# All four feed-forwards by seven block products in fixed steps, with modulation and norm work spread over three engines

## Chip, cores and metric

The kernel runs on one core of a Trainium2 chip. The metric is the device time of one execution in microseconds, median of three runs.

## What is computed

Two layers of a diffusion backbone run on 640 tokens (128 context, 512 latent) of width 1024. Cut to what matters here:

```python
def swiglu(h, w_gu, w_down):                 # w_gu 1024 x 5632, w_down 2816 x 1024
    g, u = jnp.split(h @ w_gu, 2, axis=-1)
    return (jax.nn.silu(g) * u) @ w_down
def run_layer(x, cond, lp, rope, ctx):
    mod = (jax.nn.silu(cond) @ lp['w_mod'] + lp['b_mod']).reshape(cond.shape[0], N_MOD, 1, D_MODEL)
    h = rmsnorm(x, nw[0]) * (1 + mod[:, 1]) + mod[:, 0]
    x = x + 0.5 * mod[:, 2] * swiglu(h, lp['ffn1_wgu'], lp['ffn1_wd'])
    h = rmsnorm(x, nw[1]) * (1 + mod[:, 4]) + mod[:, 3]
    out, new_ctx = token_mix(h, lp, rope, ctx)
    x = x + mod[:, 5] * out
    h = rmsnorm(x, nw[2]) * (1 + mod[:, 7]) + mod[:, 6]
    x = x + 0.5 * mod[:, 8] * swiglu(h, lp['ffn2_wgu'], lp['ffn2_wd'])
```

Each layer thus has a first feed-forward, a token mixer and a second feed-forward. The modulation vectors `mod` differ for context and latent tokens, so a segment boundary lies inside the first half of the tokens.

## The kernel before

Activations lie with features on the 128 partitions and tokens along the row, in two halves of 320 tokens; `HO = (1, 0)` makes half 1 (called p) the first and half 0 (called q, with the segment boundary) the second. Every float32 operand of a matmul is split in a rounded high part and the rest: ScalarE writes the high part (`act`), VectorE subtracts it to give the low part (`tt`), and three matmuls (high by high, high by low, low by high) stand for one product. Weights come as raw 128x512 tiles through three buffers `w`, and are split into seven pairs `wh`, `wl`.

Three of the four feed-forwards (both of layer 0, the first of layer 1) go through `ffn` (L427): two passes over 11 of the 22 hidden tiles each, gate and up projections first (8 input tiles by 3 matmuls for each of gate, up and token half), then the down projection. Beside them `mod_steps` (L348) computes modulation columns: 56 in the first feed-forward, 24 in the second, 48 in the third. A column is one 128x1024 weight row block, loaded by DMA, and two VectorE multiplications with an accumulated sum (L325, L328), one for context and one for latents. `spread` gives how many columns follow each step.

The last feed-forward goes through `ffn7` (L513). Its first `PLAIN = 2` hidden tiles are computed as above, with a down projection of their own. For the other 20, the input tiles, the two token halves and gate/up form 2x2 blocks, and seven block products of 12 matmuls each (P1, Q5, P2, Q6, Q3, Q7, Q4) take the place of eight. That needs sums of the inputs (`sums7`, on GpSimd) with their splits (`split7`), four GpSimd additions of 128x512 weights for each hidden tile, and recombinations on VectorE and ScalarE. The work is a list of steps of 12 matmuls (`order`): four hidden tiles, then a down projection of 16 steps over them, and so on. `put` hangs the work of the other engines on step numbers: a weight's load 8 steps and its split 5 steps ahead of its use. While `pin` is set, each engine keeps this program order; elsewhere a list scheduler orders instructions by its own estimate.

Between stages, `x_update` adds to the residual, `sq_tile` accumulates squares, and once the last output tile of a half is done, `norm_half` or `norm7_half` computes the reciprocal root (eight VectorE operations of 128x320) and then each of eight tiles (`norm_tile`: VectorE scale, ScalarE shift and rounding, VectorE remainder; two segments in half q). The last outputs are taken half by half (`TAIL`, `TAIL_O`), so that matmuls of q stand beside the norm of p. The tiles of class "B" are four slots of 656 values, which hold the full-precision normed half p (`xf`) and, later, two of the four raw weights of a hidden tile.

Of the kernel before, what the change touches and what calls it, by code (L numbers as in the profile page):

```python
# [104 lines left out]
class Trunk:  # L105
# [168 lines left out]
    def start(s, mc):  # L274
# [16 lines left out]
        s.h = [s.H() for _ in range(KT)]  # L291
        bm, nw = mc["sp"][:, S_OFF["bmod"][0]:S_OFF["bmod"][1]], mc["sp"][:, S_OFF["nw"][0]:S_OFF["nw"][1]]
        for f0 in range(0, KT, 4):
            fs = slice(f0, f0 + 4)
            for j in (1, 0):
# [6 lines left out]
                row = s.slots.alloc(512, False, "B")  # L302
# [13 lines left out]
            for h in HO:  # L316
                for f in range(f0, f0 + 4):
                    s.norm_tile(0, h, f, rs[h])

    def mod_cols(s, mc, j, f, pin=False):  # L320

        nc = s.nc
        l, m = mc["l"], mc["m"]
        cs = s.cs
        q = j * KT + f  # L325
        w = s.wm[q % 2]
        nc.sync.dma_start(out=w, in_=s.a["wmod"][l, q])
        i = s.stt(s.jk.ap, w, 0.5, cs[:, 0, :], ALU.mult, ALU.mult, accum_out=m[:, 0, q:q + 1])  # L328
        if pin:
            s.tc.keep_in_program_order(i)  # L330
        s.stt(w, w, 0.5, cs[:, 1, :], ALU.mult, ALU.mult, accum_out=m[:, 1, q:q + 1])
# [16 lines left out]
    def mod_steps(s, n):  # L348

        for _ in range(n):  # L350
            if s.todo:
                mc, j, f = s.todo.pop(0)
                s.mod_cols(mc, j, f, True)
                if f == KT - 1:
                    s.mod_fin(mc, j)
# [71 lines left out]
    def ffn(s, wgu, wd, i, mods, done):  # L427

        step = 0
        for hf in range(2):  # L430
            acts = [s.A(2 * T, True) for _ in range(NH)]
            w = {} if hf else {0: s.ahead}
            for mi, h in s.halves(NH, 0 if hf else HEAD, 0):
                m = hf * NH + mi
                if mi not in w:
                    w[mi] = [s.prep(wgu[m, n], KT) for n in range(2)]
                wg, wu = w[mi]
                av = acts[mi].v(2, r=True)
                sl = s.hs(h)
                g = s.proj(wg, h)  # L440
                u = s.proj(wu, h, ps=s.bank())
                t = s.norm.tile([P, H], F32, name="th", tag="tmp", bufs=4)
                s.act(t, g[:, :H], AF.Tanh, scale=0.5)
                s.stt(t, t, 1.0, g[:, :H], ALU.add, ALU.mult)
                s.tt(t, t, u[:, :H], ALU.mult)
                s.split(av[:, 0, sl], av[:, 1, sl], t)
                s.mod_steps(mods(step))
                step += 1
            if hf == 1:
                s.free(s.h)  # L450
            w = {}
            for o, h in s.halves(KT, 0, TAIL if hf else 0):
                if o not in w:
                    w[o] = s.prep(wd[o][:, hf * NH:hf * NH + NH, :], NH)
                sl = s.hs(h)
                ps = s.bank() if (2 * o + h) % 2 else s.wbank()
                s.mms(ps[:, :H], w[o], s.hl_of(acts, sl), NH)
                s.x_update(ps, i, o, h)
                if hf == 1:
                    done(o, h)  # L460
                s.mod_steps(mods(step))
                step += 1
            for a in acts:
                a.free()
# [5 lines left out]


    def norm7_half(s, i, h):

        p, q = HO
        if h == p:
            s.h = [s.H() for _ in range(KT)]
            s.xf = [s.slots.alloc(2 * H, False, "B").v(2) for _ in range(K2)]
        else:
            reg = [s.A(4 * H).v(2, 2) for _ in range(K2 // 2)]
            s.xq = [reg[k // 2][:, k % 2] for k in range(K2)]  # L480
        ps = s.bank()
        s.mm(ps[:, :H], s.ones, s.ss[h])
        r = s.norm_r(ps)
        for k in range(KT):
            t = s.norm_tile(i, h, k, r)
            f = (s.xf if h == p else s.xq)[k % K2][:, k // K2]
            for c, a, b in s.segs(h):
                o = slice(a - h * H, b - h * H)
                s.act(f[:, o], t[:, o], AF.Identity, bias=s.mB[:, c, i, k:k + 1])
# [31 lines left out]
    def ffn7(s, wgu, wd, i, mods, done):  # L521
        p, q = HO
        step = [0]

        def beside():
            s.mod_steps(mods(step[0]))
            step[0] += 1

# [3 lines left out]
        acts = [s.A(2 * T, True) for _ in range(PLAIN)]  # L532
        w = {0: s.ahead}
        n = 0
        for mi, h in s.halves(PLAIN, PLAIN, 0):
            if mi not in w:
                w[mi] = [s.prep(wgu[mi, e], KT) for e in range(2)]
            g = s.proj(w[mi][0], h)
            u = s.proj(w[mi][1], h, ps=s.bank())
            av, sl = acts[mi].v(2, r=True), s.hs(h)  # L540
            t = s.norm.tile([P, H], F32, name="th", tag="tmp", bufs=4)
            s.act(t, g[:, :H], AF.Tanh, scale=0.5)
            s.stt(t, t, 1.0, g[:, :H], ALU.add, ALU.mult)
            s.tt(t, t, u[:, :H], ALU.mult)
            s.split(av[:, 0, sl], av[:, 1, sl], t)
            if h == q:
                s.sums7(n)
                n += 1
            beside()
        w = {}  # L550
        per = WK // PLAIN
        for o in range(KT):
            if o % per == 0:
                r, (wh, wl) = s.raw(), s.hilo()
                for e in range(per):
                    s.nc.sync.dma_start(out=r[:, e * PLAIN:e * PLAIN + PLAIN, :], in_=wd[o + e][:, :PLAIN, :])
                s.split(wh, wl, r)
            for h in (q, p):
                ps = s.bank() if (2 * o + h) % 2 else s.wbank()
                xs = s.hl_of(acts, s.hs(h))  # L560
                for k in range(PLAIN):
                    e = o % per * PLAIN + k
                    s.three(ps[:, :H], (wh[:, e, :], wl[:, e, :]), xs(k), k == 0, k == PLAIN - 1)
                s.x_update(ps, i, o, h)
                beside()
            if o < K2:
                if n < K2:
                    s.sums7(n)
                    n += 1
                s.split7(o)  # L570
            else:
                k = o - K2
# [1187 lines left out]
```

## Time and profile before

| | us |
|---|---|
| runs (median, lowest, highest) | 3152.12, 3151.34, 3154.68 |
| the profiled execution, its time | 3150.53 |
| its span (first to last instruction) | 3148.7 |

The profile is one execution. An engine's busy time is the union of its instructions; matmuls overlap in the records, so a row of a matmul shows some 310 ns where the next one starts 147 ns later. Idle time of an engine that is not the bottleneck costs nothing. The stages, in us from the span's start, are: start to 52, first feed-forward to 517, mixer to 1145, second feed-forward to 1605, third to 2073, mixer to 2692, last feed-forward to the end.

### The profile page before, as it was taken

What the parts mean: (1) busy time and instruction counts of PE and PEld (TensorE: products, weight loads), DVE (VectorE), ACT (ScalarE), POOL (GpSimd) and SP (SyncE); (2) the same over time, 40 slices, a digit from 0 to 9 for tenths busy, and PEclk for the clock granted to TensorE, in tenths of its full rate; (3) what the DMA queues carried; (4) which work ended last, traced back from release to release, by engine and by line L of the source; (5) the groups of instructions that cost most, each with busy time, mean ns of one, the idle gap of its engine ahead of it and who ended that gap; (6) DMA issues with size and microseconds to landing.
All of it is one profiled execution on the core that took longest, in us unless ns stands there. A gap on an engine that the chain in (4) does not pass through costs nothing.

```text
span 3148.7 us, 54263 instructions
## 1 busy us (share of the span) xinstructions
PE 3087.9 (98%) x21206; PEld 2929.5 (93%) x21206; DVE 2136.4 (68%) x4268; ACT 1220.8 (39%) x2444; POOL 140.0 (4%) x118
## 2 busy tenths in 40 slices
PE   8999999999999999999999999999999999899999
PEld 5999998998887999999999999989989779799999
DVE  5667677757758774555566666676685687887776
ACT  4222223346544442222242223243464454444443
POOL 0000000000000000000000000000000000232221
PEclk9999999999999999999999999999999999999999
DMA  6445452454322422332323443434533224122222
GB/s 221 135 142 172 140 162 88 138 159 121 120 71 72 142 82 91 115 117 98 115 77 131 148 147 129 146 102 130 167 111 97 65 73 143 54 84 81 83 82 81
DMA packets 261468, 364.87 MB, mean 116 GB/s; under 512 B 97708, under 2 KB 143612, under 8 KB 260476
## 3 DMA queue, kind: packets, MB, share of 16 engines
q1 hardware_dynamic: 252572, 340.66, 34.1%
q10 hardware_dynamic: 8640, 20.76, 1.8%
q8 instruction: 166, 2.72, 0.4%
q14 instruction: 90, 0.74, 0.1%
HBM read 325.37 MB, written 35.96 MB: 115 GB/s over the span
## 4 chain that ended last, share of the span: by engine, by line
PE 89%; DVE 6%; ACT 3%; DMA 1%; issue 1%; SPq 0%; POOL 0%; DVEq 0%; ACTq 0%; POOLq 0%
PE wacc L188 47%; PE acc L188 42%; DVE tn L179 1%; ACT t_A L162 1%; DVE wl L171 1%; DVE t_H L179 1%; DVE t_S L1291 1%; DVE t_A L171 1%; ACT t_H L162 1%; ACT t_B L162 0%; DVE t_A L179 0%; ACT t_W L162 0%; DVE t L179 0%; ACT wh L162 0%; DMA w<-in_wd 0%
## 5 line engine op out<-in xcount | busy, mean ns | idle before, releaser
L188 PE MATMUL wacc<-t_H,wh 128*128 128x320 f32 x5248 | 1188.3, 312 | 24.5 <-ACT t_H L162 9.4
L188 PEld LDWEIGHTS wacc<-t_H,wh 128*128 128x128 f32 x5248 | 877.9, 187 | 52.5 <-DVE t_H L179 14.3
L188 PE MATMUL wacc<-t_H,wl 128*128 128x320 f32 x2624 | 812.3, 311 | 2.5 <-DVE wl L171 2.5
L162 ACT ACTIVATE wh<-w 128x512 fp32r<-128x512 f32 (+2 forms) x772 | 470.4, 613 | 746.5 <-PE wacc L188 488.3
L171 DVE TENSOR_TENSOR wl<-w,wh 128x512 fp32r<-128x512 f32 (+2 forms) x772 | 528.4, 686 | 251.0 <-ACT wh L162 245.1
L188 PE MATMUL acc<-t_H,wh 128*128 128x320 f32 x2496 | 556.6, 308 | 0.0
L188 PE MATMUL acc<-t_A,wh 128*128 128x320 f32 x2272 | 503.6, 308 | 0.2 <-DVE t_A L171 0.2
L188 PEld LDWEIGHTS wacc<-t_H,wl 128*128 128x128 f32 x2624 | 491.5, 187 | 10.3 <-issue 5.3
L188 PE MATMUL wacc<-t_A,wh 128*128 128x320 f32 x2048 | 468.2, 310 | 9.3 <-DVE tg L179 5.5
L188 PEld LDWEIGHTS acc<-t_H,wh 128*128 128x128 f32 x2496 | 418.5, 188 | 0.8 <-ACT wh L162 0.2
L188 PE MATMUL acc<-t_H,wl 128*128 128x320 f32 x1248 | 383.6, 308 | 0.0
L188 PEld LDWEIGHTS acc<-t_A,wh 128*128 128x128 f32 x2272 | 380.1, 188 | 0.8 <-DVE t_A L171 0.5
L188 PEld LDWEIGHTS wacc<-t_A,wh 128*128 128x128 f32 x2048 | 345.2, 188 | 17.3 <-DVE tg L179 6.6
L188 PE MATMUL acc<-t_A,wl 128*128 128x320 f32 x1136 | 350.0, 308 | 0.3 <-DVE wl L171 0.3
L188 PE MATMUL wacc<-t_A,wl 128*128 128x320 f32 x1024 | 317.3, 310 | 2.0 <-DVE wl L171 2.0
L188 PEld LDWEIGHTS acc<-t_H,wl 128*128 128x128 f32 x1248 | 234.0, 188 | 0.1
L188 PEld LDWEIGHTS acc<-t_A,wl 128*128 128x128 f32 x1136 | 213.3, 188 | 0.5 <-DVE wl L171 0.5
L179 DVE SCALAR_TENSOR_TENSOR t_A<-acc,mG,t_A 128x320 f32<-128x320 f32 (+1 forms) x192 | 88.4, 479 | 178.8 <-PE acc L188 173.7
L188 PEld LDWEIGHTS wacc<-t_A,wl 128*128 128x128 f32 x1024 | 192.5, 188 | 5.2 <-DVE wl L171 2.2
L171 DVE TENSOR_TENSOR th<-th,acc 128x320 f32<-128x320 f32 x136 | 66.0, 487 | 186.9 <-PE acc L188 186.9
L162 ACT ACTIVATE t_A<-th 128x320 fp32r<-128x320 f32 x176 | 82.7, 471 | 248.4 <-DVE th L171 221.6
L179 DVE SCALAR_TENSOR_TENSOR t_W<-t_W 128x1024 f32<-128x1024 f32 x128 | 156.3, 1221 | 2.1
(201 smaller groups left out, 3086.0 us busy)
## 6 DMA issues: line engine op xcount, KB each, us to landing
w<-in_wgu SPq DMA_DIRECT2D x292, 256.0 KB, 2.8
t_W<-in_wmod SPq DMA_DIRECT2D x128, 512.0 KB, 4.1
w<-in_win SPq DMA_DIRECT2D x168, 256.0 KB, 3.0
w<-in_wd SPq DMA_DIRECT2D x136, 256.0 KB, 2.8
gd<-tg SPq DMA_DIRECT2D x96, 160.0 KB, 2.2
tg<-gd SPq DMA_DIRECT2D x96, 160.0 KB, 2.3
t_B<-in_wgu SPq DMA_DIRECT2D x40, 256.0 KB, 2.8
w<-in_wd SPq DMA_DIRECT2D x48, 192.0 KB, 2.4
```

The source lines that it names most:

```text
L162: return s.order(s.nc.scalar.activation(out=out, in_=in_, func=func, **kw))
L171: return s.order(s.nc.vector.tensor_tensor(out=out, in0=a, in1=b, op=op))
L179: return s.order(s.nc.vector.scalar_tensor_tensor(out=out, in0=a, scalar=sc, in1=b, op0=op0, op1=op1, **kw))
L188: return s.order(s.nc.tensor.matmul(out, lhsT, rhs, start=start, stop=stop, **kw))
L1291: nc.vector.tensor_reduce(out=nm2.ap[:, i:i + 1], in_=ps[:, :H], axis=AX.X, op=ALU.max)
```

## The change

All four feed-forwards go through `ffn7`; `ffn` and `spread` are gone. The first one has four plain hidden tiles, with one modulation column after each of their eight steps; the others have two plain tiles. The plain tiles' own down projection is gone: the hidden tiles are grouped (0,4), (4,8), (8,12), (12,16), (16,18), (18,22), plain ones included, and each group has 16 down steps. The other modulation columns lie evenly on the fixed steps up to 12 before the last down projection, and each is now a GpSimd multiplication of 128x1024, one VectorE multiplication with a sum, and one ScalarE pass with a sum. Norms ahead of a feed-forward keep the full-precision half p back for ScalarE (`later`), and in half q VectorE multiplies by the reciprocal root alone while ScalarE scales and shifts. Some remainders of splits move from VectorE to GpSimd. Weight splits come last in a step (`late=2`), behind modulation (`late=1`).

```diff
+    def mod_cols(s, mc, j, f):
+        q = j * KT + f
+        w, m = s.wm[q % 2], mc["m"]
+        def second():
+            s.act(s.jk.ap, s.jk.ap, scale=0.5, accum_out=m[:, 1, q:q + 1])
+        return (lambda: s.dma(w, s.a["wmod"][mc["l"], q]),
+                lambda: s.mul(s.jk.ap, w, s.cs[:, 1, :]),
+                lambda: s.stt(w, w, 0.5, s.cs[:, 0, :], ALU.mult, ALU.mult, accum_out=m[:, 0, q:q + 1]),
+                second)
...
+    def norm7_tile(s, i, h, k, r):
+        x, hv = s.x[k], s.h[k].v(2, r=True)[:, :, s.hs(h)]
+        if h == HO[0]:
+            t = s.xf[k % K2][:, k // K2]
+            A, B = s.mA[:, 1, i, k:k + 1], s.mB[:, 1, i, k:k + 1]
+            s.stt(t, x[:, s.hs(h)], A, r, ALU.mult, ALU.mult)
+            s.act(hv[:, 0], t, AF.Identity, bias=B)
+            s.stt(hv[:, 1], t, B, hv[:, 0].bitcast(F32), ALU.add, ALU.subtract)
+            s.later.append(lambda: s.act(t, t, AF.Identity, bias=B))
+            return
+        t = s.xq[k % K2][:, k // K2]
+        s.tt(t, x[:, s.hs(h)], r, ALU.mult)
+        for c, a, b in s.segs(h):
+            o = slice(a - h * H, b - h * H)
+            A, B = s.mA[:, c, i, k:k + 1], s.mB[:, c, i, k:k + 1]
+            s.act(hv[:, 0, o], t[:, o], AF.Identity, scale=A, bias=B)
+            s.act(t[:, o], t[:, o], AF.Identity, scale=A, bias=B)
+        s.tt(hv[:, 1], t, hv[:, 0].bitcast(F32), ALU.subtract)
...
-        s.split(e[:, 0], e[:, 1], s.xf[k][:, 1])
+        s.act(e[:, 0], s.xf[k][:, 1])
+        s.add(e[:, 1], s.xf[k][:, 1], e[:, 0].bitcast(F32), ALU.subtract)
...
+        chunks = [range(a, b) for a, b in ((0, 4), (4, 8), (8, 12), (12, 16), (16, 18), (18, 22))]
...
+        n, end = len(s.todo), min(tails) - 12
+        for e, (mc, j, f) in enumerate(s.todo):
+            t = e * end // n
+            for fn, d in zip(s.mod_cols(mc, j, f), (0, 5, 6, 7)):
+                put(t + d, fn, late=1)
...
-            s.ffn(s.a["wgu1"][l], s.a["wd1"][l], 0, spread(len(s.todo), *(STEPS3 if l else STEPS1)), s.normed(1, s.ahead_mix(l)))
+            s.ffn7(s.a["wgu1"][l], s.a["wd1"][l], 0, PLAIN if l else 4, 0 if l else 1, s.normed(1, s.ahead_mix(l)))
-            s.mix(s.normed(2, s.ahead_ffn(s.a["wgu2"][l]), s.norm7_half if l == L - 1 else None))
+            s.mix(s.normed(2, s.ahead_ffn(s.a["wgu2"][l]), s.norm7_half))
...
-                s.ffn(s.a["wgu2"][l], s.a["wd2"][l], 2, spread(len(s.todo), *STEPS2), done)
+                s.ffn7(s.a["wgu2"][l], s.a["wd2"][l], 2, PLAIN, 0, done)
```

## Rows read from the trace of the kernel before

**Rows 1.** The page: busy time of each engine, share of the span, instructions.

```profile
PE 3087.9 (98%) x21206; PEld 2929.5 (93%) x21206; DVE 2136.4 (68%) x4268; ACT 1220.8 (39%) x2444; POOL 140.0 (4%) x118
```

**Rows 2.** Windows: the four feed-forwards; window, length, busy time (instructions), PEclk, DMA share, GB/s.

```profile
52.00:517.00 465.00, 463.39 (x3152) 462.36 (x3153) 315.06 (x605) 133.69 (x253) 1.80 (x1) 1.00 0.42 139
...
1145.00:1605.00 460.00, 460.00 (x3130) 458.99 (x3129) 248.28 (x484) 135.37 (x258) 0.00 (x0) 1.00 0.33 106
1605.00:2073.00 468.00, 466.83 (x3166) 464.40 (x3166) 309.46 (x606) 137.32 (x265) 1.80 (x1) 1.00 0.39 130
...
2700.00:3148.70 448.70, 432.18 (x2892) 427.22 (x2890) 343.08 (x580) 181.26 (x383) 127.92 (x96) 0.99 0.25 79
```

**Rows 3.** The chain that ended last: start, length, what; one projection, three block products.

```profile
74.06 3.52 PE wacc L188 x24
...
2843.83 5.28 PE wacc L188 x36
```

**Rows 4.** Windows inside the last feed-forward (PE, PEld, DVE, ACT, POOL), and one tail.

```profile
509.63:519.09 9.46, 9.15 (x60) 8.56 (x59) 8.20 (x21) 4.56 (x9) 0.00 (x0) 1.00 0.40 139
2692.18:2734.18 42.00, 34.62 (x196) 30.38 (x195) 39.01 (x76) 26.56 (x69) 14.39 (x16) 0.92 0.12 38
2734.18:2754.39 20.21, 16.39 (x98) 15.63 (x97) 18.34 (x42) 6.35 (x16) 2.77 (x2) 0.92 0.27 92
2754.39:2778.55 24.16, 21.89 (x146) 21.14 (x145) 23.75 (x28) 12.10 (x26) 15.82 (x10) 1.00 0.20 66
2803.35:2880.79 77.44, 77.44 (x531) 77.44 (x530) 58.07 (x97) 31.83 (x65) 22.44 (x16) 1.00 0.26 82
2842.07:2891.35 49.28, 49.28 (x339) 49.28 (x338) 41.06 (x61) 25.62 (x54) 16.65 (x12) 1.00 0.25 79
```

**Rows 5.** Groups by form, first feed-forward: shapes, count, busy us, mean ns, idle before.

```profile
L171 DVE TENSOR_TENSOR wl<-w,wh 128x512 fp32r<-128x512 f32 x117 | 80.5, 688 | 22.3 <-ACT wh L162 20.7
L179 DVE SCALAR_TENSOR_TENSOR t_W<-t_W 128x1024 f32<-128x1024 f32 x56 | 68.4, 1221 | 1.0
...
L162 ACT ACTIVATE t_C<-t_W 128x1024 f32<-128x1024 f32 x2 | 2.1, 1044 | 0.0
```

**Rows 6.** Groups by form in one block of the last feed-forward, 2880.79 to 2958.23.

```profile
L171 DVE TENSOR_TENSOR wl<-w,wh 128x512 fp32r<-128x512 f32 x20 | 16.1, 807 | 2.5 <-ACT wh L162 2.5
L171 DVE TENSOR_TENSOR wl<-t_B,wh 128x512 fp32r<-128x512 f32 x9 | 9.5, 1059 | 3.4 <-ACT wh L162 3.3
L171 DVE TENSOR_TENSOR wl<-t_A,wh 128x512 fp32r<-128x512 f32 x8 | 7.7, 960 | 1.3 <-ACT wh L162 1.3
L179 DVE SCALAR_TENSOR_TENSOR th<-th,tg 128x320 f32<-128x320 f32 x4 | 4.6, 1145 | 0.1
...
L171 DVE TENSOR_TENSOR acc<-tg,acc 128x320 f32<-128x320 f32 x8 | 3.9, 488 | 0.1
L171 DVE TENSOR_TENSOR t_A<-th,t_A 128x320 fp32r<-128x320 f32 x8 | 3.8, 480 | 0.0
```

**Rows 7.** Groups by form on GpSimd: one of 320 values, one of 512.

```profile
L165 POOL TENSOR_TENSOR t_B<-t_A,t_B 128x320 f32<-128x320 f32 x4 | 3.5, 867 | 0.3
...
L165 POOL TENSOR_TENSOR w<-w 128x512 f32<-128x512 f32 x1 | 1.3, 1283 | 2.4 <-DVE wl L171 2.4
```

**Rows 8.** Timeline of VectorE, then GpSimd, early in the last feed-forward: start, length, what.

```profile
2756.26 1.77 DVE L171 TENSOR_TENSOR wl<-w,wh 128x512 fp32r<-128x512 f32 x1
...
2761.36 1.78 DVE L171 TENSOR_TENSOR wl<-t_B,wh 128x512 fp32r<-128x512 f32 x1
2763.06 0.68 DVE L171 TENSOR_TENSOR wl<-w,wh 128x512 fp32r<-128x512 f32 x1
2763.66 0.68 DVE L171 TENSOR_TENSOR wl<-t_A,wh 128x512 fp32r<-128x512 f32 x1
...
2755.88 1.62 POOL L165 TENSOR_TENSOR w<-w 128x512 f32<-128x512 f32 x1 [11.61 <-DVE wl L171]
...
2760.96 1.63 POOL L165 TENSOR_TENSOR t_B<-t_B,w 128x512 f32<-128x512 f32 x1
```

More of the change, by code (lines that the diff above doesn't have):

```diff
@@ L425, in halves, with norm7_begin @@
         return o + [(t, a) for t in range(n - last, n)] + [(t, b) for t in range(n - last, n)]
[L427 to L475, printed above, removed]
+    def norm7_begin(s, h):
+        if h == HO[0]:
             s.h = [s.H() for _ in range(KT)]
             s.xf = [s.slots.alloc(2 * H, False, "B").v(2) for _ in range(K2)]
+            s.later = []
         else:
@@ L480, in norm7_half @@
             s.xq = [reg[k // 2][:, k % 2] for k in range(K2)]
+    def norm7_half(s, i, h):
+        s.norm7_begin(h)
         ps = s.bank()
@@ L519, in three, with gated, ffn7 @@
         s.mm(ps, wl, xh, False, last, skip_group_check=True)
-    def ffn7(s, wgu, wd, i, mods, done):
+    def gated(s, act, h, g, u):
+        av, sl = act.v(2, r=True), s.hs(h)
+        t = s.norm.tile([P, H], F32, name="th", tag="tmp", bufs=4)
+        s.act(t, g, AF.Tanh, scale=0.5)
+        s.stt(t, t, 1.0, g, ALU.add, ALU.mult)
+        s.tt(t, t, u, ALU.mult)
+        s.split(av[:, 0, sl], av[:, 1, sl], t)
+    def ffn7(s, wgu, wd, i, plain, mods, done):
         p, q = HO
[L523 to L527, printed above, removed]
@@ L530, in ffn7 @@
         sums = [s.A(4 * H, True).v(2, 2, r=True) for _ in range(3 * K2 // 2)]
         s.s7 = [[sums[(3 * k + j) // 2][:, (3 * k + j) % 2] for j in range(3)] for k in range(K2)]
-        acts = [s.A(2 * T, True) for _ in range(PLAIN)]
+        acts = {}
         w = {0: s.ahead}
-        n = 0
-        for mi, h in s.halves(PLAIN, PLAIN, 0):
+        todo = list(s.later) + [fn for k in range(K2) for fn in (lambda k=k: s.sums7(k), lambda k=k: s.split7(k))]
+        steps = s.halves(plain, 2, 0)
@@ L536, in ffn7 @@
+        first = 2
+        for n, (mi, h) in enumerate(steps):
             if mi not in w:
                 w[mi] = [s.prep(wgu[mi, e], KT) for e in range(2)]
+            if h == p:
+                acts[mi] = s.A(2 * T, True)
             g = s.proj(w[mi][0], h)
             u = s.proj(w[mi][1], h, ps=s.bank())
[L540 to L572, printed above, removed]
-                v = s.h[k].v(2, r=True)
-                s.split(v[:, 0, s.hs(q)], v[:, 1, s.hs(q)], s.xq[k][:, 0])
@@ L577, in ffn7 @@
-        order, chunks = [], []
-        m = PLAIN
-        while m < NM:
-            chunks.append(range(m, min(m + WK, NM)))
-            m += WK
+            s.gated(acts[mi], h, g[:, :H], u[:, :H])
+            s.mod_next(mods)
+            if n < first:
+                m = len(s.later) // first
+                for fn in todo[:m]:
+                    fn()
+                del todo[:m]
+            elif n < 4:
+                for fn in todo[:K2]:
+                    fn()
+                del todo[:K2]
@@ L585, in ffn7 @@
                 new = [(f, n) for n in ("P1", "Q5", "P2", "Q6", "Q3", "Q7")]
[L586 to L590 removed]
+                if f in begun:
+                    new = new[3:]
+                elif f > plain:
+                    new.insert(1, (f - 1, "Q4"))
                 order += new
```

97 lines of the change are left out of this document (45 added, 52 removed).

## The prediction

> **What bounds the kernel now.** First the page: TensorE is busy 98% of the span, VectorE 68%, ScalarE 39%, GpSimd 4% [rows 1]. Then the windows by stage: in the three plain feed-forwards TensorE idles 1.6, 0.0 and 1.2 us of some 465 [rows 2], so they cost what their matmuls cost. The chain gives the price: 24 matmuls in 3.52 us, 36 block-product matmuls in 5.28, so 0.1467 us each [rows 3]. A plain feed-forward has 22 x 2 x 2 x 24 + 8 x 2 x 66 = 3168 matmuls, 464.6 us; with about 2 us of waits I take 467. Then the last stage, because it already runs what the others shall run. In its steady blocks of 44 steps (four hidden tiles by seven products, 16 down steps; 528 matmuls, 77.44 us) TensorE never waits, while VectorE is busy 58.07 us [rows 4], so 19.4 us are free. They are unevenly spread: the 28 product steps (49.28 us) hold 41.06 us of VectorE and leave 8.2, the down steps leave the rest. Its head is poor: from 2692.18 to 2754.39 it takes 62.2 us for 288 matmuls (42.2), and 24.16 us for the next 144 (21.1) [rows 4]: 23 us lost.
>
> **Matmuls removed.** A hidden tile by seven products saves 12 matmuls: 18 tiles in the first feed-forward (2952 left, 433 us), 20 in the second and third (2928 left, 429.4 us): 696 matmuls, 102 us off TensorE. The whole question is whether VectorE, with the modulation now beside the block products, lets this through.
>
> **GpSimd against VectorE.** Four additions on GpSimd start at 2755.88 to 2760.96, 1.69 us apart; the four VectorE subtractions between them start at 2756.26 to 2761.36, 1.70 apart, where two of them alone are 0.60 apart (2763.06, 2763.66) [rows 8]. So two engines that both read two SBUF operands take turns, and each 512-wide addition costs a busy VectorE 1.1 us. In a steady block it costs less: against 688 ns of the form without GpSimd [rows 5] and 480 ns of its 320-wide kind, the four stretched groups lose 20 x 119 + 9 x 371 + 8 x 272 + 4 x 665 ns = 10.6 us, over 16 additions 0.66 us each. Operations with an operand in PSUM keep their 488 ns [rows 6].
>
> The Trainium skill says more (SBUF — State Buffer, § Who interferes with whom): a VectorE instruction with two SBUF inputs and a GpSimd instruction that reads SBUF exclude one another, and the second to issue waits for the whole of the first. The rows agree on who is hit, but show 1.1 and 0.66 us lost where the addition alone lasts 1.28. By that rule at its full, 2.37 us per modulation multiplication and 1.28 per addition, the time below would come out at some 3380 us.
>
> **The modulation's price.** Removed: one of two VectorE multiplications of 1.22 us a column [rows 5]. Kept: the other, 1.22. Added: a GpSimd multiplication of 128x1024. None is in the trace; from 867 ns at 320 and 1283 at 512 [rows 7] the line goes on to 2.4 us (above: 3.3, twice a stretched addition). It costs VectorE twice what an addition does, between 2 x 0.66 = 1.3 and 2 x 1.1 = 2.2; below nothing is excluded, since VectorE reads the same row as well. I take 1.7, because VectorE will seldom be idle when it comes (nearer rows 8) though a third of its operations do not collide. A column then costs VectorE 2.9 us (ends 2.5 and 3.4), more than the 2.44 of before. The ScalarE pass is 1.04 us [rows 5]; ScalarE has 31.8 of 77.44 us busy [rows 4], so it hides.
>
> First and third feed-forward: 48 columns over fixed steps. The third has 139 + 80 = 219 steps before its last down projection, so 207 carry columns, 10.2 in 44 steps: 10.2 x 2.9 = 29.6 against 19.4 free, 10.2 over; a fuller VectorE also raises the additions from 0.66 to some 0.8, 2.4 more. 12.6 x 207/44 = 59 us. The first has 205, so 193 steps, 10.9 columns: 31.7 - 19.4 + 2.4 = 14.7, x 193/44 = 65 us. VectorE keeps program order there, and the weight splits on which the next product waits stand behind the modulation in each step, so its lateness goes to TensorE once the 5 steps (8.8 us) of lead are spent. Second: 24 columns, 5.1 a block, 5.1 x 2.5 = 13 of 19.4 free; in its product steps 3.3 x 2.5 = 8.2 against 8.2 free: I allow 4 us.
>
> **Heads and tails.** The plain tiles' own down projection, 96 matmuls that lay between the norm and the first sums, is gone from the head; so are its 20.2 us. GpSimd's sums (16 of 0.9 us, 8 remainders more) and the weights that wait for the slots of `xf` now stand nearer to the first product. Against that, VectorE, busy 39.0 of 42.0 us in the old head [rows 4], does half q's norm in two operations a tile for four. A head costs between 2 us (the plain form) and 23 (the old one); I take 14 in the second, third and last, 7 in the first, whose norm lies in the start. Tails: after p's sum of squares the mixer's first matmul comes 9.46 us later, over 60 matmuls of half q [rows 4]. Now q's last two outputs are 24 matmuls, 3.5 us: 6 us open, three times (end 0 if the list scheduler finds other work, none of which is left then).
>
> SP's queue has as many modulation loads as before. Each waits for the row two columns earlier (VectorE, some 2.7 steps before), no later than its other buffers; free. A column's VectorE multiplication overwrites the row, so it waits for GpSimd, and weight splits queue behind it; GpSimd, busy 22.4 us a block and some 26 more, should be ahead: nothing, or 1.4 us each when an addition stands before it.
>
> **The sum**, on the profiled 3150.5 us: first 433 + 7 + 6 + 65 = 511 for 467, +44; second 429.4 + 14 + 6 + 4 = 453, -14; third 429.4 + 14 + 6 + 59 = 508, +41; last 429.4 + 14 for 429.4 + 23, -9. Together +62: 3212.5. The median of the runs is 1.6 us above the profiled one, so I say 3213. Own range: with a column at 2.5 and heads of 2 the terms are 34 and 29 for 65 and 59, and heads give 41 back: 3110 at the very lowest. With a column at 3.4 and the additions at 1.1: (37.1 - 19.4 + 7) x 4.39 = 108 and (34.7 - 19.4 + 7) x 4.7 = 105, the second 22: about 3320. Both ends ask for all at once; 3150 to 3290 is likely.
>
> **Rivals.**
> *VectorE keeps up.* The collisions fall into VectorE's idle time. It decides at 19.4 / 10.2 = 1.9 us a column, a loss of 0.68 to each multiplication of 2.4. For it: additions lose only half their length in the steady rows, and a column with no collision (1.22) would fit. Against it: the product steps alone have 8.2 us free for 6.5 columns, 1.26 each. Then only heads and tails remain: 446 + 449 + 449 + 443 against 3 x 467 + 453 gives 67 us less, 3085. Chance 0.27, of which 0.04 ends near no change.
> *The clock follows the waits.* TensorE's mean granted clock was 0.92 in the two broken stretches of the old head [rows 4]. If a fifth of the first and third ran at the lower level, matmuls would take 0.293 us there, and a hidden tile's 84 would last 24.6 us where VectorE needs some 14.5: 38 tiles / 5 x 10 = 76 us more, 3289. Chance 0.04: waits spread over many steps are short.
> *The order does it, not the collisions.* VectorE waits for GpSimd's product at each column, since additions that wait for weights stand before it: 96 x 1.4 = 134 us more, 3347. Chance 0.04. Then VectorE would show idle time released by GpSimd, not longer operations.
>
> **Chances.** My forecast 0.65, of which 0.03 falls near no change. Measurements of this kernel tell 0.2% (6.3 us) from nothing. Faster 0.23, same 0.07, slower 0.70. The range 3085 to 3290 leaves out the better half of the first rival and the worst ends.
>
> **What would show it.** Right: windows of the first and third feed-forward above 495 us with VectorE over 95% busy, TensorE waiting for `wl`; the group of 128x512 subtractions well over 1000 ns in the mean; block of 44 steps at 88 to 93 us. The second near 453 with blocks near 77.4. Wrong: if blocks with columns last 77 to 79 us, the price of a column is under 1.9 and the kernel is faster; if TensorE waits mostly in the heads, these were mis-sized.

## The result and the profile after

The changed kernel takes 3336.12 us (median of 4 runs, 3330.77 to 3339.18) where the kernel before takes 3153.3 (4 runs, 3151.34 to 3154.68): 1.058 times as long, 95% interval 1.056 to 1.060. The profiled execution took 3334.5 us, with a span of 3332.5. The forecast was 3213, range 3085 to 3290: the direction was right, the size was not; +62 us were foreseen and +184 came between the profiled executions.

The page, busy time of each engine (before: [rows 1]). TensorE has 696 matmuls less and is busy 92% of a longer span; VectorE went from 2136 us to 2650, GpSimd from 140 to 911.

```profile
PE 3067.5 (92%) x20510; PEld 2892.5 (87%) x20510; DVE 2650.4 (80%) x4604; ACT 1542.2 (46%) x3172; POOL 911.0 (27%) x558
```

From one first sum of squares of half p to the next, the stages moved as follows: start and first feed-forward 509.6 to 595.2 (+85.6), mixer -0.9, second feed-forward 470.2 to 493.4 (+23.2), third 469.1 to 546.5 (+77.4), mixer -2.7, last 466.0 to 467.2 (+1.3). All the time went into the three feed-forwards that now hold block products and modulation columns together.

Windows of the kernel after (window, length, then PE, PEld, DVE, ACT, POOL busy, granted clock, DMA share, GB/s): the four feed-forwards; a block of 44 steps in the first, the second, two in the third, one in the last; then the down steps and the product steps of the second of the third's blocks, the product steps of the first's and of the second's block, and the 12 matmuls after one wait in the third's. Compare [rows 2, 4].

```profile
52.00:600.00 548.00, 468.31 (x2942) 460.99 (x2941) 494.98 (x699) 244.72 (x501) 277.72 (x149) 0.92 0.36 121
1235.00:1713.00 478.00, 434.72 (x2866) 428.32 (x2864) 411.57 (x640) 222.88 (x459) 207.73 (x128) 0.96 0.31 102
1713.00:2256.00 543.00, 466.39 (x2930) 457.17 (x2930) 484.12 (x719) 249.91 (x519) 274.02 (x153) 0.93 0.34 115
2830.00:3332.00 502.00, 481.75 (x3233) 476.80 (x3231) 366.39 (x631) 207.38 (x432) 139.03 (x104) 0.98 0.25 80
...
231.20:328.80 97.60, 85.58 (x531) 84.65 (x530) 92.90 (x123) 42.92 (x87) 52.61 (x27) 0.91 0.37 124
1389.50:1474.20 84.70, 79.54 (x531) 78.83 (x530) 74.56 (x109) 36.75 (x75) 35.56 (x21) 0.98 0.32 107
1801.10:1895.88 94.78, 83.26 (x531) 81.92 (x530) 89.78 (x119) 41.55 (x84) 50.02 (x26) 0.93 0.38 128
1895.88:1989.24 93.36, 82.07 (x531) 81.14 (x530) 83.69 (x121) 41.70 (x84) 51.88 (x26) 0.95 0.36 124
3033.60:3111.00 77.40, 77.40 (x530) 77.40 (x529) 58.88 (x97) 31.71 (x64) 22.17 (x16) 1.00 0.26 82
...
1895.88:1924.04 28.16, 28.16 (x195) 28.16 (x194) 24.11 (x49) 10.70 (x19) 11.67 (x6) 1.00 0.42 135
1924.04:1989.24 65.20, 53.91 (x339) 52.98 (x338) 59.58 (x73) 30.99 (x65) 40.21 (x21) 0.92 0.34 119
259.37:328.77 69.40, 57.38 (x339) 56.45 (x337) 66.59 (x82) 31.17 (x65) 39.09 (x21) 0.88 0.34 114
1417.70:1474.18 56.48, 51.32 (x338) 50.62 (x337) 51.44 (x67) 28.01 (x59) 27.18 (x17) 0.97 0.28 94
1967.16:1970.50 3.34, 3.34 (x12) 3.34 (x13) 3.31 (x4) 1.14 (x3) 2.44 (x2) 0.50 0.77 281
```

A block without columns still lasts 77.40 us, in the last feed-forward. With 11 columns it lasts 97.6, with 10 some 94, with 5 it lasts 84.7. VectorE is busy 92.9, 89.8, 83.7 and 74.6 us of these: in the first and third more than the 77.4 that TensorE needs, in the second less, and the block is late all the same. Over the whole block VectorE is never full: 4.7, 5.0, 9.7 and 10.1 us are idle. But the down steps keep their 28.16 us, and the product steps, where TensorE needs 49.3, carry the whole delay: 69.4, 65.2 and 56.5 us in the first, third and second. There VectorE is busy 66.6, 59.6 and 51.4 us, more than 49.3 in all three; 2.8, 5.6 and 5.0 us are idle.

What TensorE waited for, in the whole kernel (us, times, longest):

```profile
PE wacc L184 <- DVE tg L167: 131.9, 46, 8.4
PE acc L184 <- ACT wh L155: 31.3, 3, 13.3
PE wacc L184 <- ACT t_H L155: 17.4, 9, 5.3
```

The first row is the wait before Q4: this product adds into the bank that holds P1, Q6 and Q7, and VectorE must have read it (`tg`) after Q7. Between Q7 and Q4 lies one step, P1 of the next tile.

What VectorE waited for in the block at 1895.88: the high part of a weight from ScalarE, a down product, GpSimd's product.

```profile
DVE wl L167 <- ACT wh L155: 4.9, 5, 1.5
DVE t_A L175 <- PE acc L184: 4.0, 8, 0.7
DVE t_W L175 <- POOL t_C L158: 1.7, 1, 1.7
```

VectorE's groups by form in the block of the first feed-forward (compare [rows 6]), then GpSimd's multiplications in the whole kernel:

```profile
L167 DVE TENSOR_TENSOR wl<-w,wh 128x512 fp32r<-128x512 f32 x21 | 28.3, 1346 | 1.9 <-ACT wh L155 1.8
L167 DVE TENSOR_TENSOR wl<-t_B,wh 128x512 fp32r<-128x512 f32 x8 | 15.8, 1974 | 0.0
L175 DVE SCALAR_TENSOR_TENSOR t_W<-t_W 128x1024 f32<-128x1024 f32 x11 | 15.4, 1396 | 0.0
...
L158 POOL TENSOR_TENSOR t_C<-t_W 128x1024 f32<-128x1024 f32 x128 | 345.4, 2698 | 279.0 <-DMA t_W<-in_wmod 131.0 <-ACT t_C L155 98.9 <-ACT wh L155 49.1
```

Subtractions that took 807 and 1059 ns take 1346 and 1974. One collision in the timeline, GpSimd, VectorE, TensorE (start, length):

```profile
1956.46 2.83 POOL L158 TENSOR_TENSOR t_C<-t_W 128x1024 f32<-128x1024 f32 x1
...
1956.97 2.67 DVE L167 TENSOR_TENSOR t_A<-th,t_A 128x320 fp32r<-128x320 f32 x1
...
1962.41 2.81 DVE L167 TENSOR_TENSOR wl<-t_B,wh 128x512 fp32r<-128x512 f32 x1
...
1966.55 0.47 DVE L167 TENSOR_TENSOR tg<-tg,wacc 128x320 f32<-128x320 f32 x1
...
1967.16 0.87 PE L184 MATMUL wacc<-t_A,wh 128*128 128x320 f32 x2 [5.60 <-DVE tg L167]
```

The subtraction of 320 values, 480 ns alone [rows 6], ends 0.35 us after the multiplication beside which it began. After a second collision, at 1962.41, VectorE comes to `tg`, and TensorE has stood still for 5.60 us; its next 12 matmuls run at the granted clock 0.50, the 1.2 GHz level, 278 ns each.

### The profile page after: what moved, and what is told of

Read it like the earlier page. It is cut to its first block, busy times and chain, and to the rows that moved or that the text cites. A ratio compares the mean times of both kernels' runs of the same rounds, so it can differ in the third digit from the quotient of the medians.

```text
span 3332.5 us, 54842 instructions
## 1 busy us (share of the span) xinstructions
PE 3067.5 (92%) x20510; PEld 2892.5 (87%) x20510; DVE 2650.4 (80%) x4604; ACT 1542.2 (46%) x3172; POOL 911.0 (27%) x558
## 4 chain that ended last, share of the span: by engine, by line
PE 62%; DVE 22%; ACT 5%; issue 5%; DMA 2%; POOL 1%; SPq 0%; DVEq 0%; ACTq 0%; POOLq 0%
PE acc L184 33%; PE wacc L184 29%; DVE wl L167 9%; DVE t_W L175 3%; DVE t_A L167 2%; DVE t_A L175 2%; DVE th L175 2%; ACT t_A L155 1%; ACT t_H L155 1%; DVE acc L167 1%; ACT wh L155 1%; DMA w<-in_wd 1%; DVE tg L167 1%; DVE t_S L1264 1%; DMA tg<-gd 1%
## 5 line engine op out<-in xcount | busy, mean ns | idle before, releaser
L184 PE MATMUL wacc<-t_H,wh 128*128 128x320 f32 (+1 forms) x4320 | 991.6, 314 | 41.0 <-ACT t_H L155 17.4
L184 PE MATMUL acc<-t_A,wh 128*128 128x320 f32 x3824 | 868.2, 314 | 38.9 <-ACT wh L155 31.3
L184 PEld LDWEIGHTS wacc<-t_H,wh 128*128 128x128 f32 (+1 forms) x4320 | 727.6, 188 | 71.8 <-ACT t_H L155 20.9
L167 DVE TENSOR_TENSOR wl<-w,wh 128x512 fp32r<-128x512 f32 (+1 forms) x718 | 637.9, 892 | 157.2 <-ACT wh L155 155.2
L184 PEld LDWEIGHTS acc<-t_A,wh 128*128 128x128 f32 x3824 | 659.6, 193 | 43.6 <-ACT wh L155 32.5
L184 PE MATMUL wacc<-t_H,wl 128*128 128x320 f32 (+1 forms) x2160 | 673.8, 313 | 12.4 <-DVE wl L167 12.4
L155 ACT ACTIVATE wh<-w 128x512 fp32r<-128x512 f32 (+1 forms) x718 | 428.9, 606 | 435.9 <-DMA w<-in_wd 154.5
L184 PE MATMUL acc<-t_A,wl 128*128 128x320 f32 x1912 | 598.5, 313 | 1.0 <-DVE wl L167 1.0
L184 PE MATMUL wacc<-t_A,wh 128*128 128x320 f32 x1888 | 465.1, 329 | 140.9 <-DVE tg L167 131.9
L184 PEld LDWEIGHTS wacc<-t_H,wl 128*128 128x128 f32 (+1 forms) x2160 | 406.5, 188 | 18.6 <-DVE wl L167 14.3
L158 POOL TENSOR_TENSOR t_C<-t_W 128x1024 f32<-128x1024 f32 x128 | 345.4, 2698 | 279.0 <-DMA t_W<-in_wmod 131.0
```

What stands on the lines that cost most here:

```text
L155: return s.order(s.nc.scalar.activation(out=out, in_=in_, func=func, **kw))
L167: return s.order(s.nc.vector.tensor_tensor(out=out, in0=a, in1=b, op=op))
L184: return s.order(s.nc.tensor.matmul(out, lhsT, rhs, start=start, stop=stop, **kw))
```

## Experiments

e1, e4, e5 and e8 leave out part of the modulation, as their expectations say. Most are single runs; runs of one kernel above lie within 0.3% of one another, so differences under some 10 us say little. Below, blocks are of 44 steps in the first, second and third feed-forward. Diffs are against the changed kernel, cut at "...".

**e1: no columns in the product steps.**

```diff
-            for fn, d in zip(s.mod_cols(mc, j, f), (0, 5, 6, 7)):
-                put(t + d, fn, late=1)
...
```

> Leaves out the modulation columns of the block products' steps (120 of the 128; their sums stay zero, so the output is not the reference's) and changes nothing else. In the changed kernel TensorE lost 91 us in the product and down steps of the first feed-forward, 32 in the second and 88 in the third, 211 us against its matmuls. If the columns are the cause, these losses go and the time is 3336 - 211 = 3125 us, and a block of 44 steps takes 77.4 us in all four feed-forwards. If the block products lose time in the first three by themselves (their order, their place behind the mixer), blocks stay well above 77.4 and the time above 3200. What is left over the matmuls is then the price of heads and tails.

Measured: 3133.17 (before, same chip: 3152.10). Windows of a block of its third feed-forward and of the heads of its first, second, third and last:

```profile
1757.10:1834.50 77.40, 77.40 (x530) 77.40 (x529) 58.52 (x101) 31.69 (x64) 22.36 (x16) 1.00 0.27 83
...
52.00:135.60 83.60, 66.78 (x409) 65.07 (x409) 61.98 (x79) 42.59 (x91) 51.69 (x33) 0.86 0.30 96
1143.40:1219.10 75.70, 60.49 (x371) 57.85 (x370) 58.56 (x88) 43.24 (x96) 47.87 (x37) 0.86 0.23 76
1600.00:1679.70 79.70, 64.99 (x397) 63.03 (x398) 61.99 (x95) 47.98 (x110) 42.83 (x36) 0.88 0.17 50
2683.00:2755.10 72.10, 58.30 (x371) 56.18 (x371) 56.99 (x84) 40.96 (x94) 43.60 (x36) 0.91 0.20 63
```

The columns cost 203 us against the median of after. Without them every block takes 77.4 us, and yet only 19 of the 102 us of matmuls come back. The heads hold the rest: at 0.1467 us a matmul (407, 371, 397 and 369 in these windows) they lose 23.9, 21.3, 21.5 and 18.0 us.

**e2: Q4 two steps later, off the largest wait.**

```diff
-                    new.insert(1, (f - 1, "Q4"))
+                    new.insert(3, (f - 1, "Q4"))
...
```

> Everything of the changed kernel is computed; only the product Q4 of a hidden tile comes two steps later inside a group of four (after P2 of the next tile, not after P1), so that VectorE has three steps and not one to read the bank after Q7. Theory 'one step of lead': VectorE was busy only 84 of 93 us in a block, and TensorE's waits sit before Q4; with more lead three of four of these waits go, blocks of the third feed-forward fall from 94.5 to 85 - 88 us, the second's from 83.3 to 78 - 79, and the time to 3210 - 3250. Rival 'VectorE is full' (each column simply costs more than is free): blocks stay within 2 us, the waits move to the weight splits, and the time stays within 15 us of 3336.

Measured: 3317.04; blocks 95.4, 83.4 and 92.2 for 97.4, 84.3 and 94.1 in the mean of after. What TensorE waits for now:

```profile
PE wacc L184 <- ACT tg L155: 102.7, 42, 4.9
...
PE wacc L184 <- DVE tg L167: 21.1, 14, 3.0
```

The time is 19 us lower and blocks are 1 to 2 us shorter, nearer to the rival than to the theory. The wait before Q4 was not the cause alone: it moved to the next link of the same bank, ScalarE's read after Q6. (A link is here the stretch between two products that add into one bank, with a read between them.) The row that tops the list of waits tells where lateness surfaces.

**e3: both multiplications of a column on VectorE.**

```diff
-                lambda: s.mul(s.jk.ap, w, s.cs[:, 1, :]),
-                lambda: s.stt(w, w, 0.5, s.cs[:, 0, :], ALU.mult, ALU.mult, accum_out=m[:, 0, q:q + 1]),
-                second)
+                lambda: s.stt(s.jk.ap, w, 0.5, s.cs[:, 1, :], ALU.mult, ALU.mult, accum_out=m[:, 1, q:q + 1]),
+                lambda: s.stt(w, w, 0.5, s.cs[:, 0, :], ALU.mult, ALU.mult, accum_out=m[:, 0, q:q + 1]))
...
```

> Both multiplications of a column on VectorE again, as two operations of 1.22 us at the place of the one; no GpSimd multiplication, no ScalarE pass. Theory 'turns at SBUF' (GpSimd's multiplication holds VectorE up by about 2 us each, and that is the lateness): VectorE's price per column goes from 1.25 + 2 to 2.6, the stretched 128x512 subtractions fall from 1042 - 1630 ns to 810 - 1060, and the time falls by 40 to 90 us, to 3245 - 3295. Rival 'one step of lead': 2.6 us in one piece in VectorE's queue delays the read after Q7 about as much as before; the time stays within 25 us of 3336.

Measured: 3293.66, 42 us faster than after. A block of the first (11 columns):

```profile
223.40:317.50 94.10, 83.66 (x530) 82.47 (x529) 85.75 (x145) 31.24 (x64) 24.08 (x16) 0.93 0.40 129
```

VectorE does twice the multiplications and is busy 85.8 us where it was 92.9 with GpSimd's help: (85.75 - 58.5) / 11 = 2.5 us a column for 3.1.

**e4 and e5: the two parts of a column alone**, GpSimd's multiplication (e4), VectorE's (e5).

```diff
-            for fn, d in zip(s.mod_cols(mc, j, f), (0, 5, 6, 7)):
+            for fn, d in zip(s.mod_cols(mc, j, f)[:2], (0, 5)):      # e4
+            for fn, d in zip(s.mod_cols(mc, j, f)[::2], (0, 6)):     # e5
```

> Of each column in the product steps only the load and GpSimd's multiplication stay; VectorE's own multiplication and ScalarE's pass are left out (the sums stay zero, so the output is not the reference's). It prices the collisions alone. 'Turns at SBUF': 120 multiplications by some 2 us of VectorE still make a large part of the 211 us: loss 90 - 140 us, time 3215 - 3265. Rival 'VectorE's own 1.22 us is what is too much': loss under 50 us, time under 3175.

> Left out: GpSimd's multiplication and ScalarE's pass of the 120 columns of the product steps (their latent sums stay zero); the load and VectorE's multiplication of 1.22 us stay. With e1 (no columns, 3133) and e4 (GpSimd's part alone, 3234) it splits the column. Theory 'turns': a column's own VectorE time is 10.9, 5.5 and 10.2 x 1.22 = 13.3, 6.7 and 12.4 us a block against 18.9 free, and no turn is added, so blocks stay at 77.4 to 79 and the time comes out at 3133 to 3150. Rival 'lead': what counts is how late VectorE runs at a link of one step, whoever made it late; then 71 us of VectorE in a block costs nearly what 74 us cost in e4: blocks 81 to 84 in the first and third, 3165 to 3200.

Measured: e4 3233.64 (before: 3152.10), e5 3169.89 (before: 3155.94). A block of the third feed-forward of e4, then of e5:

```profile
1828.30:1914.10 85.80, 79.62 (x531) 78.93 (x530) 73.98 (x101) 31.36 (x65) 48.23 (x26) 0.98 0.40 135
```

```profile
1778.50:1858.90 80.40, 77.95 (x530) 77.45 (x529) 71.18 (x121) 31.92 (x64) 23.38 (x16) 1.00 0.45 145
```

In e4 VectorE executes no more instructions than in e1 and is busy 73.98 us for 58.52: ten multiplications on GpSimd cost it 1.55 us each, more than the 1.22 that they took off it. In e5, without these multiplications on GpSimd, turns alone would have left blocks of 77.4 to 79; those of the first and third take 81.8 and 80.5 in the mean, as the rival said. So there is lateness without these collisions, although VectorE has 6 us to spare in the 77.4 of a block. In the product steps of this block it has none: they hold 49.03 us of VectorE, where TensorE needs 49.3, and take 52.24.

```profile
1806.66:1858.90 52.24, 49.79 (x338) 49.29 (x337) 49.03 (x73) 25.28 (x53) 19.70 (x14) 1.00 0.46 151
```

The loads, which e5 keeps and e1 leaves out, hardly enter: ScalarE waits 9.1 us for loaded down weights in e5's block and 8.7 in e1's.

**e6 and e7: the two faults of order, one at a time.** e6 gives each link of the bank two steps or more; e7 gives a down step twice the columns of a product step.

```diff
-                    new.insert(1, (f - 1, "Q4"))
+                    new.insert(4, (f - 1, "Q4"))
...
-                order += [(g, "P1")] + [(f, "Q4")] * (f >= plain) + [(g, "Q5"), (g, "P2")]
+                order += [(g, "P1"), (g, "Q5")] + [(f, "Q4")] * (f >= plain) + [(g, "P2"), (g, "Q6")]
...
```

```diff
+        at2 = [t for t in range(end) for _ in range(2 if len(order[t + 6]) == 5 else 1)]
...
-            t = e * end // n
+            t = at2[e * len(at2) // n]
...
```

> Nothing left out: the same work, with the products of a hidden tile in another order (P1, Q5, P2, Q6, Q4 of the tile before, Q3, Q7; ahead of a group's 16 down steps P1, Q5, Q4, P2, Q6), so that between two products that add into the same bank, with a read of it in between, lie two, two and four steps, where after has three, one and one and e2 had three, one and four. Theory 'lead': most of the waits of after and of e2 sit at a link of one step; with two steps everywhere VectorE may run 3.5 us late before TensorE waits, blocks of the first, second and third fall from 97.5, 84 and 94 to 86-90, 78-80 and 84-88, time 3215 to 3260. Rival 'VectorE is full where the products are' (product steps hold 41.06 + 6.5 x 2.56 = 57.7 us of it in 49.3): lateness of 8 us in each run of product steps passes any lead of two steps, blocks stay above 92, 82 and 90, time 3290 to 3325.

> Nothing left out: the order of after, but columns are given to steps by weight, two for a down step and one for a product step (by the step of the VectorE multiplication), so that a block's 28 product steps get 4.7 of 10 columns, not 6.5, and its 16 down steps 5.3, not 3.7; VectorE then has 53 us to do in 49.3 and 30.7 in 28.2. Theory 'full where the products are': the lateness in the product steps falls from 8.4 to 3.7 us a block, blocks from 97.5, 84 and 94 to 89-92, 78-80 and 86-89, time 3240 to 3280. Rival 'lead' (VectorE is late by more than one step either way): time 3315 to 3340.

Measured: 3314.00 and 3324.48 (before: 3155.94), little for either, and each in the range of its rival. (Between Q7 and Q4 e2 has three steps, not the four that e6's expectation gives it.) What TensorE waits for in e6:

```profile
PE acc L184 <- DVE wl L167: 52.4, 28, 5.4
PE wacc L184 <- DVE tg L167: 40.8, 12, 5.7
PE acc L184 <- ACT wh L155: 34.1, 7, 12.1
PE wacc L184 <- ACT tg L155: 34.1, 20, 3.9
```

The waits spread over weights and both links, and blocks of the second still take 83.4 us in the mean (84.3 in after), in e7 82.0. Neither fault alone carries the loss.

**e9 and e11: both mended**, with the column as in after (e9) and on VectorE alone as in e3 (e11). The diffs are those of e6 and e7, with that of e3 for e11.

> Nothing left out: the order of e6 (two, two and four steps) and the columns by weight of e7 together. In after, e3, e4, e5, e6 and e7 a block of 44 steps lasts as long as VectorE is busy in it and 8 to 10 us more (83.7 and 93.4 in after, 81.9 and 92.2 in e6, 83.7 and 91.7 in e7, 71.2 and 80.4 in e5). Theory 'VectorE cannot use those 9 us, in whatever order': blocks of the first and third stay at 91 to 96, time 3300 to 3318. Rival 'each of e6 and e7 mended only one of two faults of the order, and both together let VectorE fill up': idle of 5 us or less, blocks 86 to 90, time 3250 to 3285.

> Nothing left out: e9 with both multiplications of a column on VectorE (no GpSimd or ScalarE in it), as e3 against after. e3: blocks 93, 82.7 and 90.5, VectorE busy 82.1 of 90.6. Theory 'VectorE cannot use 9 us': the waits for GpSimd's product go, the rest stays, blocks 88 to 92, time 3270 to 3295. Rival 'the order makes the idle': blocks 84 to 87, time 3225 to 3260.

Measured: e9 3281.62, e11 3236.37 (before: 3155.47, 13 runs). A block of the second and of the first in e9, then the same in e11:

```profile
1363.10:1442.00 78.90, 78.01 (x531) 77.49 (x530) 69.28 (x109) 36.62 (x74) 36.38 (x21) 1.00 0.33 105
227.00:319.00 92.00, 81.19 (x531) 79.09 (x530) 85.31 (x121) 43.01 (x87) 53.62 (x27) 0.98 0.41 134
```

```profile
1349.80:1428.10 78.30, 77.62 (x529) 77.36 (x528) 70.35 (x119) 31.78 (x64) 23.85 (x16) 1.00 0.36 115
221.40:309.70 88.30, 80.16 (x531) 78.80 (x530) 83.99 (x142) 30.57 (x64) 24.93 (x16) 0.98 0.39 130
```

Here the two causes part. In the second the block falls from 84.7 to 78.9 and 78.3: what was lost there was order, of products and columns together. In the first, VectorE's own 84 to 85 us are over the 77.4 in this order too. The gain of e9 lies in VectorE's busy time and not in its idle time: with the same work it is busy 85.3 us for 92.9 in the first (idle 6.7 for 4.7) and 69.3 for 74.6 in the second (idle 9.6 for 10.1). So what a column costs VectorE depends on the order; the likely reason, fewer of its operations beside one of GpSimd, was not tested alone. Without GpSimd's multiplications, from e3 to e11, the order takes 4.4 us off a block of the first in the mean, 1.7 of it busy and 2.7 idle time.

e9 gains 54 us where e6 and e7 gained 22 and 12: more than their sum, and the time is in the range of its rival. Its blocks are not: 91.1 and 92.4 us in the mean of the first and third, with 5.5 and 8.3 idle, as the theory had them. e11's time is its rival's; its blocks of the first and third, 88.7 and 87.3, are above the 84 to 87 that the rival gave.

**e12: no program order in the fixed steps.**

```diff
-            s.pin = t < min(tails)
+            s.pin = False
```

> Nothing left out: after, but in the fixed steps no engine keeps the program order; the list scheduler orders by its own estimate, which knows nothing of turns between GpSimd and VectorE. Theory 'VectorE's 9 us lie in the chain from TensorE over ScalarE to VectorE and back, not in the order written': 3310 to 3360. Rival 'the fixed order makes the idle': under 3290.

Measured: 3430.34, outside both. It tells little on the idle time, since the list scheduler drew columns forward: all 72 of layer 1 into the second feed-forward. The first of these windows is there, the second is a block of the third, now without a column:

```profile
1352.00:1485.00 133.00, 93.56 (x520) 89.32 (x519) 125.68 (x153) 55.89 (x109) 89.85 (x40) 0.86 0.44 142
1959.10:2039.10 80.00, 78.27 (x531) 77.46 (x530) 59.91 (x96) 31.91 (x64) 22.38 (x16) 1.00 0.26 80
```

Even with VectorE busy 59.9 us of 80.0, the scheduler's order makes a block 2.6 us longer.

**e13: TensorE does P1 twice** in the first and third feed-forward.

```diff
+        twice = n > 24
...
-                for k in range(K2):
+                for k in [*range(K2)] * (2 if twice and n == "P1" else 1):
```

> Nothing left out, and something added: in the first and third feed-forward TensorE does product P1 of every hidden tile twice (the second pass starts the sum anew), 18 + 20 times 12 matmuls, 456 x 0.1467 = 66.9 us of work that nobody needs, right ahead of the wait before Q4. Theory 'VectorE's order and load set the blocks with columns, TensorE's waits and its matmuls at the 1.2 GHz level are only what is left over': the extra work fits in the waits, blocks stay at 97 and 94, 3330 to 3350; if the lower level itself costs time, even less, since TensorE pauses less: 3300 to 3325. Rival 'TensorE's own time is on the path all along': blocks grow by 4 x 1.76 = 7 us, 3390 to 3405.

Measured: 3327.62 (before: 3152.89). A block of the first feed-forward, and what TensorE waits for:

```profile
229.30:325.20 95.90, 86.75 (x579) 85.81 (x578) 92.85 (x125) 42.80 (x87) 54.95 (x27) 0.98 0.39 127
```

```profile
PE wacc L184 <- DVE tg L167: 87.3, 44, 6.9
```

48 matmuls more in the block, and it is not longer (97.6 in after); 67 us of added work cost nothing. The waits shrank from 131.9 to 87.3 us and the granted clock in the block rose from 0.91 to 0.98, which paid for a part: TensorE's busy time grew by only some 3 us a block in the first (84.1 to 87.2 in the mean) and 4 in the third (83.1 to 86.9). Those blocks became 1.3 and 1.9 us shorter all the same, so TensorE's busy time is not what sets the blocks with columns. What the lower clock costs by itself the run does not tell, since work and clock changed together.

**e8: the remainders of e back on VectorE**, without columns.

```diff
-        s.act(e[:, 0], s.xf[k][:, 1])
-        s.add(e[:, 1], s.xf[k][:, 1], e[:, 0].bitcast(F32), ALU.subtract)
+        s.split(e[:, 0], e[:, 1], s.xf[k][:, 1])
...
```

> Left out: the 120 columns of the product steps (their sums stay zero), as in e1, so that only heads and tails are left over the matmuls; and the four remainders of e in split7 go back from GpSimd to VectorE, which undoes one part of the change. In e1 GpSimd does 16 sums, four remainders of v and then four of e one after another, and the slots in which U1 and U2 are loaded come free with the last of them; products start at 1186.9 in the second feed-forward. Theory 'GpSimd's chain sets the head': the slots come free 4 to 9 us earlier in the second, third and last, 0 to 5 in the first: 3105 to 3120, against 3133 of e1. Rival 'VectorE or the loads set it': within 5 us of 3133.

Measured: 3125.87, 7 us under e1, between the two forecasts and within what single runs may differ by; 2.2, 1.9, 1.0 and 0.7 of these lie in the four feed-forwards, where the theory wanted 4 to 9 in three of them. GpSimd's first sum of weights in the second, in e1 and then in e8:

```profile
1184.95 1.26 POOL L158 TENSOR_TENSOR w<-t_B 128x512 f32<-128x512 f32 x1 [1.86 <-DMA t_A<-in_wgu]
```

```profile
1179.70 1.29 POOL L158 TENSOR_TENSOR w<-t_B 128x512 f32<-128x512 f32 x1 [4.33 <-DMA t_A<-in_wgu]
```

Counted from the stage's start (1125.84 and 1121.34) it comes at 59.1 and 58.4 us: VectorE, with the four remainders more, finishes about when GpSimd did. GpSimd's chain alone doesn't set the head.

**e10: seven products only where no column is.** The second feed-forward stays plain and takes all 72 columns of layer 1; the third runs by block products. The diff is cut, and against the kernel before; `ffn7` is that of the changed kernel with e8's remainders.

```diff
-                s.todo = [(mc, j, f) for j in range(MOD2) for f in range(KT)]
+                s.todo = [(mc, j, f) for j in range(9) for f in range(KT)]
...
-            s.ffn(s.a["wgu1"][l], s.a["wd1"][l], 0, spread(len(s.todo), *(STEPS3 if l else STEPS1)), s.normed(1, s.ahead_mix(l)))
+            if l == 0:
+                s.ffn(s.a["wgu1"][l], s.a["wd1"][l], 0, spread(len(s.todo), *STEPS1), s.normed(1, s.ahead_mix(l)))
+                s.mod_end()
+            else:
+                s.ffn7(s.a["wgu1"][l], s.a["wd1"][l], 0, PLAIN, 0, s.normed(1, s.ahead_mix(l)))
```

> Nothing left out: the kernel before, but the 7-product form is used where no column is computed: the second feed-forward stays plain and takes all 72 columns of layer 1 (before: 24 there, 48 in the third), and the third becomes seven products without columns, with the remainders of e on VectorE as in e8. VectorE in the plain second: 248 us and 48 x 2.44 more, 365 of 460 us, which leaves 95 idle; TensorE should not wait there (460 to 472 between the sums of squares, before 470). The third: 458.7 in e8 for 469.1 before, 10 less; last 465.1 for 466.0. Theory: 3138 to 3146, faster than before by 0.2 to 0.45%. Rival (72 columns on 56 of the plain form's steps make TensorE wait, or the norm ahead of the third waits for the first columns): 3150 or more.

Measured: 3147.62 (10 runs, 3142.57 to 3150.69) against 3155.47 for the kernel before (13 runs): ratio 0.9975, interval 0.9965 to 0.9984. Of the versions that leave nothing out it is the one that is faster than both kernels, by 0.25% against the kernel before. That is the gain forecast; the time itself lies just over the 3138 to 3146 given. The plain second with its 72 columns:

```profile
1147.93:1600.20 452.27, 452.16 (x3077) 451.07 (x3076) 349.34 (x681) 131.55 (x252) 1.81 (x1) 1.00 0.50 159
```

TensorE has no wait there; 48 columns more are free. The third falls from 469.1 to 460.5 us, the last from 466.0 to 465.2.

## Why the prediction was right and wrong

*Right: the matmuls saved and the blocks without columns.* 696 matmuls are gone, and the blocks of the last feed-forward and of e1 take 77.4 us.

*Right: a column's price on VectorE.* Forecast 2.9 us (ends 2.5 and 3.4), for GpSimd's part 1.7 (1.3 to 2.2). Measured 1.5 for GpSimd's part (e4), and for a column 3.1 in the first, 2.5 to 3.1 in the third, 2.5 to 3.2 in the second; in e9's order 2.4 in the first. For the first feed-forward the sum of VectorE's work, 58.1 + 31.7 + 2.4 = 92.2 us a block, met 92.9; in the third the forecast held 90.0 and 86.7 came in the mean. The Trainium skill's rule (SBUF — State Buffer, § Who interferes with whom: the ports that VectorE and GpSimd share are an exclusive lock, and whoever issues first has them for the whole instruction) is seen in single collisions, as in the timeline at 1956.46. In the mean the rows give less: 1.5 us lost for each multiplication of 2.7 us. The rows show one reason, that operations which read PSUM keep their time (`acc<-tg,acc` 483 ns beside the columns, 488 without); how often VectorE had nothing to do when the multiplication came was not counted.

*Wrong: "19.4 us are free".* I set the block at VectorE's work without a gap, and counted its idle time of a block without columns as free to the last. Rows of after show 4.7 us idle in the first, 5 to 10 in the third, 10 in the second, about half of it in product steps, beside a TensorE that waits, and the rest in the down steps, which are not late. So a block came 5.4 us over the forecast in the first (97.4 for 92.1), 4.1 in the third (94.1 for 90.0), 6 in the second (84.3 for about 78): over the stages, 88, 28 and 87 us for 65, 4 and 59, together 75 of the 122 us that the forecast missed.

*Wrong: "once the 5 steps of lead are spent".* That lead is the weights'. Of the links of the bank that Q6, Q7 and Q4 add into, the last two have one step, so TensorE waits there after the first microseconds of lateness (131.9 us for `tg`, 15 for `wl`). That VectorE's idle time comes of these short links is not shown: in product steps it mostly waits for a weight's high part (3.4 of the 5.6 us idle in those at 1924.04), and two steps at each link alone (e6) gained 22 us. The second feed-forward shows best what order costs: 28 us lost against e1, of which e9 wins back 22 (blocks of 78.9). Unevenness has its share: the product steps had 8.2 us free for 6.5 columns. I wrote that down as an argument against a rival, and then averaged over the block in my own sum. By the same prices the product steps alone give the first a block of nearly the same length (41.06 + 7 x 2.9 + 2.4 = 63.8 us and 28.2 of down steps); what came there is 66.6 us of VectorE and 2.8 idle, while the down steps gave nothing back.

*Wrong: heads and tails.* Forecast 7, 14, 14 and 14 us for the heads and 6 for three tails, 67 together. e1 shows 23.9, 21.3, 21.5 and 18.0 for heads; the tails lose some 9 us each there, about 112 together. Without columns the kernel should have come out 66 us faster and came out 17 to 19 faster: 49 us, the other part of the miss. The bound of 23 from the old head was the right row; I took 14 and 7 between two bounds with no row for them. What holds the heads is not settled: e8 excludes GpSimd's chain as the only cause.

*The rivals.* "VectorE keeps up" is out: its point was 1.9 us a column. "The clock follows the waits": the clock did fall, and TensorE lost 69 us over its matmuls that way beside 142 us of waits in product and down steps; but in e13 67 us of matmuls more did not lengthen these stages, so TensorE's busy time was not what set them. "The order does it" named VectorE's waits for GpSimd's product; that wait is 1.7 us of the block at 1895.88. The order was at fault all the same, in another place than any rival had.

*The signs.* Stages over 495 us and subtractions over 1000 ns came. VectorE over 95% came in no whole stage (90 and 89%), and in the first feed-forward's blocks just so (95%). TensorE waited for the bank, not for `wl`; the blocks, at 94 and 97 us, were over the 88 to 93 given.

*Open:* how the 4 to 9 us of VectorE's idle time that are left in e9 and e11 could be used (in the first's blocks it waits 3.2 us for GpSimd's product, 2.1 for weights' high parts and 1.4 for down products in e9, 2.6 for high parts and 1.1 for down products in e11); how much of e9's gain is fewer collisions; what sets the heads.

## To carry to other kernels

An engine that keeps program order can set the time before it is full: here 71 us of VectorE beside 77.4 of TensorE made a block of 80.4 (e5). Count its free time by the shortest stretch over which it may be late (here the product steps), and for that look through every accumulator's links, not only the weights' lead. Work given to GpSimd beside a VectorE that reads two SBUF operands may cost VectorE more than it takes off; price it there first. And an added piece of useless work (e13) is a quick way to see whether an engine's waits are the cause or what is left over; look at the clock as well, since it may change with the work.

## What the runs showed of the hardware

As forecast, a multiplication given to GpSimd (2698 ns in the mean) costs VectorE more than doing it: 1.55 us lost for 1.22 saved (e4), and 42 us of the kernel (e3). I had not expected that this cost depends so much on the order of the same work: VectorE's busy time in a block of the first fell from 92.9 to 85.3 us (e9). Nor that after a wait of 5.60 us the next 12 matmuls run at the granted clock 0.50, 278 ns each for 147, while 48 matmuls more in a block bring that clock back to 0.98 without making the block longer (e13).
